# Sums over partitions in the attention heads: from TensorE to GpSimd, with GpSimd's short operations moved to VectorE

## The chip, the cores and the metric

The kernel runs on one core of a Trainium2 chip. The metric is the device time of one execution in microseconds (us); the median of several runs is given, and one more execution was profiled. The engines are TensorE (PE, matrix products), VectorE (DVE), ScalarE (ACT), GpSimd (POOL) and SyncE (SP, which issues most DMA transfers). Each has its own queue of instructions, worked off in order, and waits on the others through semaphores.

## The reference

One layer of a hybrid encoder step, for 512 prompt frames and 64 sample frames (T = 576 in all), in float32. What the change touches is the normalisation of queries and keys in eight attention heads of 128 channels, and the inverse roots of the other norms:

```python
def rmsnorm(x, g):
    y = xf * lax.rsqrt(jnp.mean(xf * xf, axis=-1, keepdims=True) + EPS) * g
...
hn = rmsnorm(x, g_norm1)
proj = hn @ w_in
q, k, v, gb, gc, hc = jnp.split(proj, ...)
q = rmsnorm(q.reshape(B, T, N_HEADS, HEAD_DIM), g_q)
k = rmsnorm(k.reshape(B, T, N_HEADS, HEAD_DIM), g_k)
...
o_attn = stick_breaking_blocks(q, k_all, v_all, P)
u = gc * hc
o_conv = gb * conv3(u)
mix = concat([rmsnorm(o_attn, g_attn_out), rmsnorm(o_conv, g_conv_out)])
x = x + mix @ w_out
x = x + (silu(h2 @ w_gate) * (h2 @ w_up)) @ w_down
```

## The kernel before

Activations lie with channels on the 128 partitions and frames along the row. The 576 frames are worked on in two halves of 288 (`HALVES`, `HALF`). For precision each float32 operand of a product is split into a high and a low part (`split`, line 221: a cast on ScalarE, then a subtraction on VectorE), and a product is three matmuls (`step`, line 210). A product over D = 2048 channels for one half is 16 steps of three matmuls (`product`, line 215). After each step a clock of the program ticks (`pipe.tick()`), and work that was put off until that tick is issued (`Pipeline`, line 66): a generator that yields n goes on n ticks later.

The program has the input stage, then the eight heads (`head`, line 805), then two groups of the convolution in the plain form, the rest in a form with fewer products, the output projection and the feed-forward part. A head projects q, k and v one after the other (`project`, line 489), each for both halves. `norm_evac` (line 619) takes a half of q or k out of PSUM: it multiplies by the row scale R1 into `E` (line 637), squares it on ScalarE (line 640), splits the square, and 13 ticks later (16 for k, 6 and more in head 0) sums it over the partitions by two matmuls with a matrix of ones (`channel_sums`, lines 468 to 472), so that each partition has the sum. `rsqrt_mean` (lines 456 to 466) makes the inverse root of it: the mean plus epsilon on VectorE (461), Ln and Exp on ScalarE (462, 463), and one Newton step of three VectorE operations (464 to 466). Line 629 then scales `E`, and the result is split for the score matmuls.

When both halves of k are there, `attend` (line 660) starts 15 ticks later: scores into the tiles `z` (679), softplus (653 to 656), masks (688), block sums (691, 696), cumulative sums by triangular matmuls, weights (717, 719), the values' product `po` (747), the same for the sample frames with short operations on 64 columns (752 to 758), and at the end the squares of the head's output are added into `acc_a` (`add_squares`, line 504). The masks, block sums, short operations and the adding of squares are on GpSimd. The tile `sq` has two buffers, `hl` (which the split square uses) two.

The weights of the next products are split two products ahead (`next_weight`, line 194; lines 175 and 176); the one numbered 2 is split by GpSimd. In head 0 the evacuation of both halves of q and of k comes at one time, since the row scale R1 is only then known.

TensorE's order is the program's, written by hand. The order on ScalarE, VectorE and GpSimd within the heads is made by the framework's planner from the program's order and its own estimate of costs.

`rsqrt_mean` is also called for the scale of the heads' output (`head_forms`), for that of the groups (`group_scale`) and for the second norm (`row_scale2`), two halves each.

Of the kernel before, what the change touches and what calls it, by code (L numbers as in the profile page):

```python
# [3 lines left out]

# [6 lines left out]
F32 = mybir.dt.float32  # L11
# [5 lines left out]
P = 128  # L17
# [77 lines left out]
def tile_hybrid_stream_step(  # L95
# [89 lines left out]
    def split_weight(lo_eng):  # L185
        raw = raws[len(ready)]
        n = specs[len(ready)][1] * specs[len(ready)][2]
        hi, lo = weight_split(len(ready))
        for a in range(0, n, 1024):
            weight_parts(raw, hi, lo, a, a + 1024, lo_eng)  # L190
# [3 lines left out]
    def next_weight():  # L194
        i = pos[0]
        pos[0] += 1
        end = first_out if i < first_out else first_block
        while len(raws) < min(i + 2, end):
            load_weight()
        while len(ready) < min(i + 2, end):  # L200
            split_weight(nc.gpsimd if i == 2 else nc.vector)
        while len(raws) < min(i + 3, end):
            load_weight()
        out = ready[i]
        ready[i] = None
        return out
# [18 lines left out]
    def parts(name):  # L225
        t = tmp.tile([P, 2, HALF], F32R, tag="hl", name=name)
        return t[:, 0], t[:, 1]
# [225 lines left out]

    hpool.release()

    def rsqrt_mean(dst, src, n, width, ms=None, t=None):
        if ms is None:
            ms = tmp.tile([P, HALF], F32, tag="ms", name="ms", bufs=1)[:, :width]
            t = tmp.tile([P, HALF], F32, tag="t", name="t", bufs=1)[:, :width]
        y = tmp.tile([P, HALF], F32, tag="y", name="y")[:, :width]  # L460
        nc.vector.tensor_scalar(out=ms, in0=src, scalar1=1.0 / n, scalar2=EPS, op0=ALU.mult, op1=ALU.add)
        nc.scalar.activation(out=y, in_=ms, func=AF.Ln)
        nc.scalar.activation(out=y, in_=y, func=AF.Exp, scale=-0.5)
        nc.vector.tensor_tensor(out=t, in0=y, in1=y, op=ALU.mult)
        nc.vector.scalar_tensor_tensor(out=t, in0=t, scalar=-0.5, in1=ms, op0=ALU.mult, op1=ALU.mult)
        nc.vector.scalar_tensor_tensor(out=dst, in0=t, scalar=1.5, in1=y, op0=ALU.add, op1=ALU.mult)

    def channel_sums(src_hi, src_lo, a, b, name):
        ps = misc(name)[:, : b - a]
        mm(ps, oner, src_hi, start=True, stop=False)  # L470
        mm(ps, oner, src_lo, start=False, stop=True)
        return ps
# [28 lines left out]
            else:  # L501
                defer.append((evac, ps, a, b))

    def add_squares(acc, src, first):
        if first:
            nc.scalar.activation(out=acc, in_=src, func=AF.Square)
        else:
            sq = tmp.tile([P, HALF], F32, tag="sq", name="sqm")
            nc.scalar.activation(out=sq, in_=src, func=AF.Square)
            nc.gpsimd.tensor_tensor(out=acc, in0=acc, in1=sq, op=ALU.add)  # L510

    turns = {}

# [53 lines left out]
    def group_scale(acc, dst, rows_of):  # L567

        four = cpool.tile([P, 2, 2, HALF], F32R, tag="uc", name="sqg")
        for i, (a, b) in enumerate(HALVES):  # L570
            sh, sl = four[:, i, 0], four[:, i, 1]
            split(sh, sl, acc[:, a:b])
            yield rows_of
            ss = channel_sums(sh, sl, a, b, "ssg")
            ms, t = (tmp.tile([P, HALF], F32, tag=tag, name=tag + "g") for tag in ("r", "sq"))
            rsqrt_mean(dst[:, a:b], ss, 8 * P, HALF, ms, t)
            yield rows_of

    acc_a = rpool.tile([P, T], F32, tag="R", name="acc_a", bufs=2)
# [39 lines left out]
    def norm_evac(name, gcol, dst_f, dst_hi, dst_lo, first, after=None):  # L619
        E = t1.tile([P, T], F32, tag="E", name=f"E{name}", bufs=2)  # L620

        def rest(a, b, sh, sl):
            if first:
                lags[0] += 4
            yield 6 + lags[0] if first else 16 if after else 13
            ss = channel_sums(sh, sl, a, b, "ss")
            r = tmp.tile([P, HALF], F32, tag="r", name="r")
            rsqrt_mean(r, ss, P, HALF)
            nc.vector.scalar_tensor_tensor(out=dst_f[:, a:b], in0=E[:, a:b], scalar=gcol, in1=r,
                                           op0=ALU.mult, op1=ALU.mult)  # L630
            e = min(b, TP)
            split(dst_hi[:, a:e], dst_lo[:, a:e], dst_f[:, a:e])
            if after and b == T:
                pipe.spawn(after)

        def evac(ps, a, b):
            nc.vector.tensor_tensor(out=E[:, a:b], in0=ps, in1=R1[:, a:b], op=ALU.mult)
            sq = tmp.tile([P, HALF], F32, tag="sq", name="sq")
            sh, sl = parts("sq")
            nc.scalar.activation(out=sq, in_=E[:, a:b], func=AF.Square)  # L640
            split(sh, sl, sq)
            pipe.spawn(rest(a, b, sh, sl))

        return evac

# [14 lines left out]
    def attend(h, st):  # L660
# [20 lines left out]
        for b in (2, 1, 0):  # L681
            parts = (2, 3) if b == 2 else (b,)
            w = full[b]
            for i in parts:
                scores(i)
            softplus(pr[b][:, :w], z[b][:, :w], pr[b][:, :w])
            for i in parts:
                nc.gpsimd.tensor_tensor(out=pb[i][:, :P], in0=pb[i][:, :P], in1=m01, op=ALU.mult)
            split(ph[b][:, : width[b]], pl[b][:, : width[b]], pr[b][:, : width[b]])
            if b == 2:  # L690
                nc.gpsimd.tensor_tensor(out=pb[2][:, P:], in0=pb[2][:, P:], in1=pb[3], op=ALU.add)
                s1h = t1.tile([P, 256], F32R, tag="s1h", name="s1h")
                s1l = t1.tile([P, 256], F32R, tag="s1l", name="s1l")
                split(s1h, s1l, pb[2])
            if b == 1:
                nc.gpsimd.tensor_tensor(out=pb[1][:, P:], in0=pb[1][:, P:], in1=pb[2], op=ALU.add)
                s0h = t1.tile([P, 384], F32R, tag="s0h", name="s0h")
                s0l = t1.tile([P, 384], F32R, tag="s0l", name="s0l")
                split(s0h, s0l, pb[1])
# [49 lines left out]

        sp = t1.tile([P, T], F32, tag="pr0", name="sp")  # L750
        softplus(sp[:, :320], zc, sp[:, :320])
        nc.gpsimd.tensor_tensor(out=sp[:, 256:320], in0=sp[:, 256:320], in1=s01, op=ALU.mult)
        sh = t1.tile([P, T], F32R, tag="ph0", name="sph")
        sl = t1.tile([P, T], F32R, tag="pl0", name="spl")
        sums = sp[:, 320:]
        nc.gpsimd.tensor_copy(sums[:, 192:256], sp[:, 256:320])
        for b in (2, 1, 0):
            nc.gpsimd.tensor_tensor(out=sums[:, b * TS : (b + 1) * TS], in0=sums[:, (b + 1) * TS : (b + 2) * TS],
                                    in1=sp[:, (b + 1) * TS : (b + 2) * TS], op=ALU.add)
        split(sh, sl, sp)  # L760
        yield 18
# [16 lines left out]
        nc.scalar.copy(out=o_attn[h][:, TP:], in_=os_[:, TS:P])  # L778
        for a, b in HALVES:
            yield 3  # L780
            add_squares(acc_a[:, a:b], o_attn[h][:, a:b], h == 0)

    def values(h, st, Ev):
        yield 5
# [1063 lines left out]
```

## Time and profile before

| | us |
|---|---|
| median of 3 runs | 2372.15 |
| lowest and highest of them | 2371.21, 2373.49 |
| the profiled execution's own time | 2373.26 |
| its span, from the first to the last instruction | 2371.6 |

The mean granted TensorE clock in the profiled execution is 0.999 of full speed.

In rows of a timeline the first number is the start and the second the length in us. In rows of groups the two numbers behind the bar are the busy time of the group in us and the mean of one instruction in ns, and behind the second bar stands the idle time of the engine just before them with what ended it. Matmuls overlap one another in their pipeline: a row says 0.29 us for one of 288 columns, while a new one starts about every 0.13 us.

### The profile page before, as it was taken

The page shows a single profiled execution, that of the slowest core. Times are in us where ns is not written, and L with a number is a line of the kernel's source. Part 1 is how long each engine was busy: PE and PEld are TensorE (multiplying, and loading weights), DVE is VectorE, ACT ScalarE, POOL GpSimd, SP SyncE. Part 2 cuts the span into 40 slices and gives each one's busy share as a digit, 9 for nine tenths or more (in the row PEclk, how much of TensorE's full clock was granted, in tenths as well). Part 3 has the DMA queues.
Part 4 walks back from the last instruction along what each step waited for, and adds up shares of the span by engine and source line. Part 5 has one row for each costly group of instructions (what it writes and reads, how often), then busy time and mean ns, then how long its engine had stood idle before and what let it go on. Part 6 is the DMA issues. An engine that isn't in the chain of part 4 may idle for free.

```text
span 2371.6 us, 44043 instructions
## 1 busy us (share of the span) xinstructions
PE 2348.9 (99%) x17653; PEld 2338.0 (99%) x17653; DVE 1927.6 (81%) x2892; ACT 1166.2 (49%) x2083; POOL 290.5 (12%) x386
## 2 busy tenths in 40 slices
PE   8999999999999999999999999999999999999999
PEld 8999999999999999999999999999999999999999
DVE  7868776788887889888888888888888778887876
ACT  6656655444444555444444444444444444444444
POOL 2111111332111230000000000000000002431211
PEclk9999999999999999999999999999999999999999
DMA  8465554683368654444444444444444936886642
GB/s 259 127 179 165 138 148 111 219 263 118 109 235 220 195 166 147 140 152 135 138 152 136 138 152 137 137 152 137 137 152 132 359 112 213 224 225 199 205 131 82
DMA packets 563845, 395.75 MB, mean 167 GB/s; under 512 B 67006, under 2 KB 552760, under 8 KB 563640
## 3 DMA queue, kind: packets, MB, share of 16 engines
q1 hardware_dynamic: 554296, 376.39, 50.6%
q0 software_dynamic: 8624, 16.22, 3.4%
q8 instruction: 138, 2.26, 0.4%
q14 instruction: 67, 0.55, 0.1%
q10 hardware_dynamic: 720, 0.33, 0.0%
HBM read 301.45 MB, written 91.44 MB: 166 GB/s over the span
## 4 chain that ended last, share of the span: by engine, by line
PE 90%; DVE 5%; DMA 2%; ACT 2%; issue 1%; POOL 0%; ACTq 0%; SPq 0%; DVEq 0%; POOLq 0%
PE psy L1532 34%; PE psw L1532 17%; PE pj L213 12%; PE psx L1532 8%; PE psy L1036 6%; PE pjo L213 4%; PE psw L1036 3%; PE psx L1036 2%; DMA raw_a<-in_w_down_dram 1%; DVE whl L223 1%; PE po L747 1%; PE z L679 1%; DVE whl L1008 0%; PE os L777 0%; DMA raw_a<-in_w_in_dram 0%
## 5 line engine op out<-in xcount | busy, mean ns | idle before, releaser
L1532 PE MATMUL psy<-h_s,whl 128*128 128x288 f32 x2787 | 413.5, 295 | 0.3 <-ACT part L1542 0.3
L213 PE MATMUL pj<-x,whi 128*128 128x288 f32 x1856 | 389.9, 297 | 0.3 <-DVE x L356 0.2
L1532 PEld LDWEIGHTS psy<-h_s,whl 128*128 128x128 f32 x2787 | 384.8, 189 | 0.6 <-ACT part L1542 0.5
L223 DVE TENSOR_TENSOR whl<-raw_a,whl 128x1024 fp32r<-128x1024 f32 (+4 forms) x296 | 321.1, 1086 | 61.3 <-ACT whl L222 60.4
L1532 PE MATMUL psw<-t,whl 128*128 128x288 f32 x2400 | 348.3, 295 | 0.0
L1532 PEld LDWEIGHTS psw<-t,whl 128*128 128x128 f32 x2400 | 327.5, 188 | 0.0
L222 ACT CAST whl<-raw_a 128x1024 fp32r<-128x1024 f32 (+4 forms) x296 | 267.8, 906 | 115.2 <-issue 35.4
L213 PEld LDWEIGHTS pj<-x,whi 128*128 128x128 f32 x1856 | 304.1, 189 | 1.5 <-DVE x L356 1.0
L213 PE MATMUL pj<-x,wlo 128*128 128x288 f32 x928 | 274.1, 295 | 0.1
L223 DVE TENSOR_TENSOR whl<-raw_b,whl 128x1024 fp32r<-128x1024 f32 (+5 forms) x190 | 201.6, 1061 | 69.2 <-ACT whl L222 68.1
L222 ACT CAST whl<-raw_b 128x1024 fp32r<-128x1024 f32 (+5 forms) x190 | 165.1, 871 | 167.8 <-issue 73.4
L1542 ACT COPY part<-psy 128x288 f32<-128x288 f32 x242 | 96.6, 399 | 281.4 <-PE psy L1532 279.6
L1532 PE MATMUL psy<-b22m,whl 128*128 128x288 f32 x1212 | 183.3, 295 | 0.2 <-ACT part L1542 0.2
L1532 PE MATMUL psy<-t2t,whl 128*128 128x288 f32 x1212 | 182.9, 294 | 0.0
L213 PEld LDWEIGHTS pj<-x,wlo 128*128 128x128 f32 x928 | 174.5, 188 | 0.7 <-DVE wlo L423 0.3
L1532 PE MATMUL psx<-h_s,whl 128*128 128x288 f32 x1185 | 173.6, 294 | 0.0
L1532 PEld LDWEIGHTS psy<-b22m,whl 128*128 128x128 f32 x1212 | 168.2, 188 | 0.4 <-ACT part L1542 0.4
L1532 PEld LDWEIGHTS psy<-t2t,whl 128*128 128x128 f32 x1212 | 167.9, 188 | 0.0
L1532 PEld LDWEIGHTS psx<-h_s,whl 128*128 128x128 f32 x1185 | 162.3, 188 | 0.0
L222 ACT CAST whl<-s 128x1024 fp32r<-128x1024 f32 (+5 forms) x81 | 72.2, 892 | 102.2 <-PE psw L1532 100.9
L1311 POOL DMA_DIRECT2D hid_dram<-form x3 | 2.3, 751 | 947.6 <-DVE form L223 947.6
L1532 PE MATMUL psy<-t,whl 128*128 128x288 f32 x576 | 107.7, 297 | 0.0
(471 smaller groups left out, 4408.7 us busy)
## 6 DMA issues: line engine op xcount, KB each, us to landing
hid_dram<-form SPq DMA_DIRECT2D x147, 288.0 KB, 2.3
raw_a<-in_w_in_dram SPq DMA_DIRECT2D x41, 1024.0 KB, 5.8
raw_a<-in_w_gate_dram SPq DMA_DIRECT2D x22, 1024.0 KB, 6.0
raw_a<-in_w_up_dram SPq DMA_DIRECT2D x22, 1024.0 KB, 5.7
raw_b<-in_w_gate_dram SPq DMA_DIRECT2D x22, 1024.0 KB, 6.7
raw_b<-in_w_up_dram SPq DMA_DIRECT2D x22, 1024.0 KB, 7.0
h_s<-hid_dram SPq DMA_DIRECT2D x10, 2016.0 KB, 12.5
raw_a<-in_w_out_dram SPq DMA_DIRECT2D x16, 1024.0 KB, 5.6
```

What stands on the lines that cost most here:

```text
L213: mm(ps, w_[:, k, csl], x_, start=(k == 0 and n == 0), stop=(k == nk - 1 and n == 2))
L222: nc.scalar.copy(out=hi, in_=src)
L223: (lo_eng or nc.vector).tensor_tensor(out=lo, in0=src, in1=hi.bitcast(F32), op=ALU.subtract)
L679: mm(zb[i], a_[:, kk], b_[:, q0:TP], start=(n == 0), stop=False, skip_group_check=True)
L747: mm(po[:, i * P : 512], a_[:, i, :], b_[:, : 512 - i * P], stop=(i == 0 and n == 2), **kw)
L1036: mm(ps, whl[:, w_, j, :], x_, start=(start and j == 0 and q == 0), stop=(j == m - 1 and q == 2), skip_group_check=True)
L1311: q.dma_start(out=hid_dram[fp][2 * n - 2 : 2 * n].rearrange("f p t -> p f t"), in_=t.bitcast(F32))
L1532: mm(ps, whl[:, w_, j, :], x_, start=(start and j == 0 and q == 0), stop=(j == len(xs_) - 1 and q == 2), skip_group_check=True)
L1542: nc.scalar.copy(out=t, in_=st["y"])
```

## The change

The sum of squares over the partitions in `norm_evac` is no longer made from split squares by two matmuls: GpSimd's `partition_all_reduce` adds the squares of a half (128 partitions by 288 columns, float32) over the partitions, right after ScalarE's square, and writes the sum to every partition of an SBUF tile in the tag `hl`. The split of the square is left out. The lags of 13, 16 and 6 ticks stay.

The masks, the block sums, the short operations on sample frames, and the adding of squares at the end of a head go from GpSimd to VectorE, and so does the one weight split. The memset of `ws` stays on GpSimd, and so does the adding of squares for the convolution groups.

`rsqrt_mean` leaves out line 461: Ln takes the sum itself, with the scale 1/n and epsilon as a bias, and the Newton step is written with the sum in place of the mean. Its first operation becomes one with a scalar between the two operands.

```diff
-            split_weight(nc.gpsimd if i == 2 else nc.vector)
+            split_weight(nc.vector)
...
+    epsc = rpool.tile([P, 1], F32, name="epsc")
+    nc.vector.memset(epsc, EPS)
+
-    def rsqrt_mean(dst, src, n, width, ms=None, t=None):
-        if ms is None:
-            ms = tmp.tile([P, HALF], F32, tag="ms", name="ms", bufs=1)[:, :width]
+    def rsqrt_mean(dst, src, n, width, t=None):
+        if t is None:
             t = tmp.tile([P, HALF], F32, tag="t", name="t", bufs=1)[:, :width]
         y = tmp.tile([P, HALF], F32, tag="y", name="y")[:, :width]
-        nc.vector.tensor_scalar(out=ms, in0=src, scalar1=1.0 / n, scalar2=EPS, op0=ALU.mult, op1=ALU.add)
-        nc.scalar.activation(out=y, in_=ms, func=AF.Ln)
+        nc.scalar.activation(out=y, in_=src, func=AF.Ln, scale=1.0 / n, bias=epsc)
         nc.scalar.activation(out=y, in_=y, func=AF.Exp, scale=-0.5)
-        nc.vector.tensor_tensor(out=t, in0=y, in1=y, op=ALU.mult)
-        nc.vector.scalar_tensor_tensor(out=t, in0=t, scalar=-0.5, in1=ms, op0=ALU.mult, op1=ALU.mult)
+        nc.vector.scalar_tensor_tensor(out=t, in0=y, scalar=-0.5 / n, in1=y, op0=ALU.mult, op1=ALU.mult)
+        nc.vector.scalar_tensor_tensor(out=t, in0=src, scalar=n * EPS, in1=t, op0=ALU.add, op1=ALU.mult)
         nc.vector.scalar_tensor_tensor(out=dst, in0=t, scalar=1.5, in1=y, op0=ALU.add, op1=ALU.mult)
...
-    def add_squares(acc, src, first):
+    def add_squares(acc, src, first, eng=nc.gpsimd):
...
-            nc.gpsimd.tensor_tensor(out=acc, in0=acc, in1=sq, op=ALU.add)
+            eng.tensor_tensor(out=acc, in0=acc, in1=sq, op=ALU.add)
...
-        def rest(a, b, sh, sl):
+        def rest(a, b, ss):
...
-            ss = channel_sums(sh, sl, a, b, "ss")
...
         def evac(ps, a, b):
             nc.vector.tensor_tensor(out=E[:, a:b], in0=ps, in1=R1[:, a:b], op=ALU.mult)
             sq = tmp.tile([P, HALF], F32, tag="sq", name="sq")
-            sh, sl = parts("sq")
             nc.scalar.activation(out=sq, in_=E[:, a:b], func=AF.Square)
-            split(sh, sl, sq)
-            pipe.spawn(rest(a, b, sh, sl))
+            ss = tmp.tile([P, HALF], F32, tag="hl", name="ss")
+            nc.gpsimd.partition_all_reduce(ss, sq, P, bass_isa.ReduceOp.add)
+            pipe.spawn(rest(a, b, ss))
...
-                nc.gpsimd.tensor_tensor(out=pb[i][:, :P], in0=pb[i][:, :P], in1=m01, op=ALU.mult)
+                nc.vector.tensor_tensor(out=pb[i][:, :P], in0=pb[i][:, :P], in1=m01, op=ALU.mult)
...
-                nc.gpsimd.tensor_tensor(out=pb[2][:, P:], in0=pb[2][:, P:], in1=pb[3], op=ALU.add)
+                nc.vector.tensor_tensor(out=pb[2][:, P:], in0=pb[2][:, P:], in1=pb[3], op=ALU.add)
...
-                nc.gpsimd.tensor_tensor(out=pb[1][:, P:], in0=pb[1][:, P:], in1=pb[2], op=ALU.add)
+                nc.vector.tensor_tensor(out=pb[1][:, P:], in0=pb[1][:, P:], in1=pb[2], op=ALU.add)
...
-        nc.gpsimd.tensor_tensor(out=sp[:, 256:320], in0=sp[:, 256:320], in1=s01, op=ALU.mult)
+        nc.vector.tensor_tensor(out=sp[:, 256:320], in0=sp[:, 256:320], in1=s01, op=ALU.mult)
...
-        nc.gpsimd.tensor_copy(sums[:, 192:256], sp[:, 256:320])
+        nc.vector.tensor_copy(sums[:, 192:256], sp[:, 256:320])
         for b in (2, 1, 0):
-            nc.gpsimd.tensor_tensor(out=sums[:, b * TS : (b + 1) * TS], in0=sums[:, (b + 1) * TS : (b + 2) * TS],
+            nc.vector.tensor_tensor(out=sums[:, b * TS : (b + 1) * TS], in0=sums[:, (b + 1) * TS : (b + 2) * TS],
...
-            add_squares(acc_a[:, a:b], o_attn[h][:, a:b], h == 0)
+            add_squares(acc_a[:, a:b], o_attn[h][:, a:b], h == 0, nc.vector)
```

`group_scale` calls the shorter `rsqrt_mean` with one scratch tile less.

More of the change, by code (lines that the diff above doesn't have):

```diff
@@ L574, in group_scale @@
             ss = channel_sums(sh, sl, a, b, "ssg")
-            ms, t = (tmp.tile([P, HALF], F32, tag=tag, name=tag + "g") for tag in ("r", "sq"))
-            rsqrt_mean(dst[:, a:b], ss, 8 * P, HALF, ms, t)
+            t = tmp.tile([P, HALF], F32, tag="sq", name="sqg")
+            rsqrt_mean(dst[:, a:b], ss, 8 * P, HALF, t)
             yield rows_of
```

1 line of the change is left out of this document (added).

## The prediction

> **What bounds the kernel now.** I read the page first, then the time per head, then the engines inside one head, then single instructions.
>
> ```profile
> span 2371.6 us, 44043 instructions
> PE 2348.9 (99%) x17653; PEld 2338.0 (99%) x17653; DVE 1927.6 (81%) x2892; ACT 1166.2 (49%) x2083; POOL 290.5 (12%) x386
> ```
>
> TensorE (PE) is the bound of the whole. The change touches the eight heads, about 46 to 420 us. One head is read off the chain of waits, from the score matmuls of one head to those of the next (first column start, second length, us), and the busy times from the view of stretches over five such heads:
>
> ```profile
> 258.03 1.23 PE z L679 x6
> ...
> 305.82 1.23 PE z L679 x6
> ```
>
> ```profile
> 258.03:305.82 47.79, 47.79 (x357) 47.43 (x357) 36.02 (x70) 28.97 (x62) 7.41 (x14) 1.00 0.52 140
> ...
> sum 238.97, PE 238.97 PEld 237.16 DVE 181.34 ACT 145.48 POOL 34.10; mean PE 47.79 PEld 47.43 DVE 36.27 ACT 29.10 POOL 6.82
> ```
>
> A head is 47.8 us and PE is busy in all of it, at the full clock (1.00). VectorE (DVE) works 36.3 us of it and idles 11.5, GpSimd (POOL) works 6.8. So a matmul taken out of a head is worth its full slot, and DVE has 11.5 us a head before it takes PE's place.
>
> **The two engines get in each other's way.** These rows of the timeline carry the forecast (start, length, engine, line):
>
> ```profile
> 49.77 4.99 POOL L176 TENSOR_TENSOR wlo<-raw_a,whi 128x1024 fp32r<-128x1024 f32 x2 [10.02 <-ACT whi L175]
> ...
> 50.70 0.46 DVE L461 TENSOR_SCALAR ms<-ss 128x288 f32<-128x288 f32 x1 [1.98 <-PE ss L471]
> ...
> 52.49 2.58 DVE L464 TENSOR_TENSOR t<-y 128x288 f32<-128x288 f32 x1
> ...
> 57.98 0.45 DVE L464 TENSOR_TENSOR t<-y 128x288 f32<-128x288 f32 x1
> ```
>
> ```profile
> 293.46 1.22 DVE L176 TENSOR_TENSOR wlo<-raw_a,whi 128x1024 fp32r<-128x1024 f32 x1
> ...
> 293.81 1.53 POOL L510 TENSOR_TENSOR acc_a<-acc_a,sqm 128x288 f32<-128x288 f32 x1 [5.64 <-ACT sqm L509]
> ...
> 294.59 1.06 DVE L464 TENSOR_TENSOR t<-y 128x288 f32<-128x288 f32 x1
> ```
>
> L464 multiplies two SBUF operands. Alone it takes 0.45 us. At 52.49, with two GpSimd instructions under way until 54.76, it took 2.58 us and ended at 55.07, just behind them. At 293.81 the GpSimd add met a running VectorE subtraction, took 1.53 us, and the next L464 then waited for the add (1.06 us). L461, which reads PSUM, ran at 50.70 inside the same GpSimd work in its usual 0.46 us. So a VectorE instruction with two SBUF inputs and a GpSimd instruction run one after the other, each waiting for the whole of the other. A GpSimd sum over partitions reads SBUF too, and here it is four times a head.
>
> The Trainium skill ("SBUF — State Buffer", section "SBUF: two separate sides") says the same: the port pair the two engines share is an exclusive lock held for a full instruction, against VectorE operations with two SBUF inputs. The rows above agree for GpSimd's elementwise operations; no run so far shows it for a sum over partitions.
>
> **How much of VectorE's work can be held up.** From the groups by line over those five heads, the rows whose operation reads PSUM or has one input only:
>
> ```profile
> L461 DVE TENSOR_SCALAR ms<-ss 128x288 f32<-128x288 f32 x20 | 9.1, 453 | 3.2 <-PE ss L471 3.2
> L656 DVE SCALAR_TENSOR_TENSOR pr<-z,pr 128x384 f32<-128x384 f32 (+1 forms) x15 | 8.4, 583 | 0.7 <-ACT pr L655 0.7
> ...
> L717 DVE SCALAR_TENSOR_TENSOR z<-z,acA 128x128 f32<-128x128 f32 x20 | 6.0, 298 | 11.0 <-PE z L726 9.0 <-PE z L732 1.9
> ...
> L785 DVE STREAM_TRANSPOSE Ev<-Ev 128x576 f32<-128x576 f32 x6 | 4.7, 779 | 0.2
> L832 DVE TENSOR_TENSOR Ev<-pj,R 128x288 f32<-128x288 f32 x10 | 4.5, 453 | 6.5 <-PE pj L213 6.5
> L637 DVE TENSOR_TENSOR Ek<-pj,R 128x288 f32<-128x288 f32 x10 | 4.5, 453 | 1.1 <-PE pj L213 1.1
> L637 DVE TENSOR_TENSOR Eq<-pj,R 128x288 f32<-128x288 f32 x10 | 4.5, 448 | 0.0
> ...
> L710 DVE STREAM_TRANSPOSE kb<-kf 128x576 f32<-128x576 f32 x5 | 3.9, 778 | 0.2
> ...
> L803 DVE STREAM_TRANSPOSE kcT<-cK 128x512 f32<-128x512 f32 x5 | 3.5, 709 | 2.2 <-PE zs L705 2.2
> ...
> L769 DVE TENSOR_TENSOR ws<-cz,zc 128x320 f32<-128x320 f32 x5 | 2.4, 479 | 0.0
> ```
>
> They sum to 51.5 us, 10.3 a head. The other 36.3 - 10.3 = 26.0 us a head read two SBUF operands.
>
> **The change part by part.**
>
> *Matmuls out.* Each of the 32 sums (8 heads, q and k, two halves) loses two matmuls. In the timeline the pair starts at 50.24 and the next matmul behind it at 50.50:
>
> ```profile
> 50.24 0.29 PE L470 MATMUL ss<-sq,oner 128*128 128x288 f32 x1
> ...
> 50.50 0.29 PE L213 MATMUL pjz<-x,whi 128*128 128x288 f32 x1
> ```
>
> 0.26 us a pair, 1.04 a head, 32 x 0.26 = 8.3 us: all that PE can gain. The 32 casts on ScalarE that go with them lie beside PE (ScalarE 29.1 of 47.8 us) and count nothing.
>
> *VectorE out and in.* Per head it loses four subtractions and four L461, and takes what GpSimd did:
>
> ```profile
> L223 DVE TENSOR_TENSOR sq<-sq 128x288 fp32r<-128x288 f32 x20 | 11.5, 577 | 2.4 <-ACT sq L222 2.3
> ...
> L607 DVE TENSOR_TENSOR o_ob<-o_ob 128x288 f32<-128x288 f32 x5 | 2.3, 455 | 0.1
> ...
> L770 DVE SCALAR_TENSOR_TENSOR ws<-ws,acA 128x64 f32<-128x64 f32 x5 | 1.1, 213 | 0.0
> ```
>
> ```profile
> L688 POOL TENSOR_TENSOR pr<-pr,acA 128x128 f32<-128x128 f32 x20 | 9.6, 501 | 20.4 <-DVE pr L656 20.4
> L510 POOL TENSOR_TENSOR acc_a<-acc_a,sqm 128x288 f32<-128x288 f32 x10 | 9.1, 911 | 75.5 <-ACT sqm L509 75.5
> L758 POOL TENSOR_TENSOR sp<-sp 128x64 f32<-128x64 f32 x15 | 5.0, 330 | 1.2
> ```
>
> Out: 4 x 0.577 + 4 x 0.453 = 4.1 us. In, priced by VectorE's rows of the same width: four masks and one add of 128 columns at 0.30 (L717), one add of 256 at 0.42 (between L717 and L607), five of 64 at 0.21 (L770), two adds of 288 at 0.455 (L607): 3.9 us. VectorE stays at 36.1 us a head, but its two-input work goes from 26.0 to 26.0 - 2.3 + 3.9 = 27.6. The squaring L464 becomes one of the same kind and length. The weight split that head 0 gave GpSimd (4.99 us) is two VectorE instructions of 1.2 us; it ends L464's wait of 2.1 us, so nought. The six other inverse roots (heads' and groups' scales, R2) lose one L461 each, 6 x 0.45 = 2.7 us at most; VectorE has other work there and I count zero.
>
> *The sum over partitions.* No row has it. The nearest is L510, one GpSimd pass over 128x288 in 0.91 us: the lower bound, since every column is read and written at least once. From above, GpSimd's slowest operation here is a power worked out in software:
>
> ```profile
> 38.53 1.21 POOL L441 TENSOR_TENSOR rst<-ssr,nhalf 128x5 f32<-128x5 f32 x1 [12.10 <-DVE ssr L439]
> ```
>
> 1.21 us for 5 columns is 0.24 a column, 70 us for 288: the upper bound. I take a value near L510's end, since it only adds: 128 rows are folded to one in seven halvings, at a pass of 0.91 us each 6.4 us. I call it X = 6.4, an estimate.
>
> The Trainium skill's figure that speaks against it ("GPSIMD Engine Reference", section "3.2 Cross-partition — where GPSIMD wins") is 247.7 us for a reduction along partitions of 128x2048, so 34.8 us for 288 columns by an estimate from that page, and it is for another instruction; by it a head would be 27.6 + 4 x 34.8 = 167 us and the time about 3330 us. No trace shows it yet.
>
> *What waits.* GpSimd's queue in a head holds nothing else but a memset, so nothing is stuck behind the sums there. Who waits is VectorE, by the lock, and behind it ScalarE's casts, the weight splits and PE. If lock and work pack without a gap, a head is 27.6 + 4 x 6.4 = 53.2 us. If instead the sums fall at chance, only the share of a head without two-input work, (47.8 - 26.0)/47.8 = 46%, is free to run beside them, and a head is 47.8 - 1.0 + 0.54 x 25.6 = 60.6 us. ScalarE's and VectorE's order is the planner's, and where it puts the readers of a sum I can't see; a reader put too early holds its whole engine. I take the middle, 56.9, 9.1 above today, for eight heads 73 us. Cover and lateness: without the lock the sums would mostly hide, since the program leaves time for them:
>
> ```profile
> 268.36 0.44 ACT L640 ACTIVATE sq<-Eq 128x288 f32<-128x288 f32 x1 [1.89 <-DVE Eq L637]
> ...
> 291.33 0.45 ACT L640 ACTIVATE sq<-Ek 128x288 f32<-128x288 f32 x1
> ```
>
> ```profile
> 273.31 0.46 DVE L461 TENSOR_SCALAR ms<-ss 128x288 f32<-128x288 f32 x1 [0.44 <-PE ss L471]
> ...
> 299.11 0.44 DVE L461 TENSOR_SCALAR ms<-ss 128x288 f32<-128x288 f32 x1
> ```
>
> From the square's end to L461 there are 4.5 us for the first half of q and 7.3 for the last of k. In head 0 four squares come together, the first at 46.7; the last L461 is at 62.6, and the view of waits shows PE already short of k there:
>
> ```profile
> 46.73 0.81 ACT L640 ACTIVATE sq<-Eq 128x288 f32<-128x288 f32 x2 [6.81 <-DVE Eq L637]
> ...
> 62.60 0.45 DVE L461 TENSOR_SCALAR ms<-ss 128x288 f32<-128x288 f32 x1
> ```
>
> ```profile
> PE z L679 <- ACT kh L222: 2.0, 1, 2.0
> ```
>
> Four sums in a row, 25.6 us, in these 16 us make head 0 late by some 10 us, about as much as the others lose; it is counted as one of the eight.
>
> **Sum.** The profiled execution took 2373.3 us (span 2371.6 and 1.7 around it), the median of the runs is 2372.15. 2373.3 + 73 = 2446; against the median 2445. I forecast 2445, slower.
>
> **Rivals.** (a) *The sum is short*, X of about 3 us or less: 27.6 + 12 fits into 46.8 us, it lies in VectorE's idle time, and the heads shrink by the matmuls: 2372 - 8.3 = 2364. For it: GpSimd passes of 0.9 us, and 4.5 to 7.3 us of room. Against: three passes are few for 128 rows, and a head's chain has VectorE steps behind each other. The point from which it turns is 0.54 x 4X = 1.0 + what VectorE's idle time absorbs, near X = 3 to 4. (b) *The lock doesn't hold for this instruction*, or X is just at that point: then only q's first half is late (6.4 against 4.5 us) and head 0 waits (25.6 us of sums in a room of about 16 us), giving back what the matmuls gave: 2368 to 2377. For it: the lock is shown for elementwise operations only. (c) *The sum goes column by column* and GpSimd itself is the bound, above X = 12, where 4X exceeds 47.8 us. At X = 16 a head is 27.6 + 64 = 91.6 us, plus 44 each: 2372 + 350 = 2722. For it: the power's 0.24 us a column; against: a power is dear arithmetic, a sum isn't.
>
> **Chances.** Forecast (lock, X about 4 to 12, 2380 to 2600 by the same two formulas): 0.52. (a) 0.25. (b) 0.08. (c) 0.15. What a measurement of this kernel tells from no change is 0.2%, 4.7 us. So faster 0.25, same 0.08, slower 0.67. The range must take in (a), since the other sign holds a quarter: 2362 to 2600; it leaves out (c) and little else. The likeliest case alone: 2380 to 2600.
>
> **What would show it.** The row of the sum on GpSimd, 32 times, gives X directly: 6.4 expected. VectorE's two-input rows (L464's successor, the weight splits of 1.2 us) should have means some us above their 0.45 and 1.2 where a sum runs, and PSUM readers (the multiplication out of PSUM, 0.45) should not. A head between score matmuls should be about 57 us, with PE waiting for VectorE or ScalarE; the time behind 450 us should be unchanged. Wrong would be: X under 3 us with heads of 46.8 us; or X of 6 us with VectorE's means unchanged, which would mean that there is no lock for this instruction; or GpSimd busy in all of a head.

## The result and the profile after

| | before | after |
|---|---|---|
| median of 4 runs (us) | 2372.82 | 2406.2 |
| lowest and highest | 2371.21, 2374.73 | 2404.51, 2409.49 |
| ratio after / before | | 1.014, 95% interval 1.0128 to 1.0153 |
| span of the profiled execution | 2371.6 | 2405.3 |

The change makes the kernel slower by 33.4 us. The forecast had the sign, and more than twice the size (73 us); that the sign was right was luck, as the account of the prediction below shows. First the page of the kernel after:

```profile
span 2405.3 us, 43819 instructions
...
PE 2356.3 (98%) x17589; PEld 2344.3 (97%) x17589; DVE 1939.5 (81%) x2927; ACT 1160.1 (48%) x2051; POOL 304.5 (13%) x314
```

TensorE still bounds it, with 64 matmuls fewer, as meant; but it has 33.7 us more of span and only 7.4 us more of busy time. So most of the loss is time in which TensorE stands still, and some is matmuls that are each a little longer. Where it lies can be read off the first and last starts of the matmuls of one line (view by source line; the three numbers before the range are the shortest, median and longest duration in ns). Before, the convolution and the feed-forward part:

```profile
L1036 PE MATMUL psy<-x,whl x624: 292/294/398, 486.0 to 691.0; 128*128 128x288 f32 x156
...
L1036 PE MATMUL psy<-forms,whl x384: 290/294/399, 691.1 to 782.5; 128*128 128x288 f32 x192
```

```profile
L1532 PE MATMUL psy<-h_s,whl x2787: 290/294/445, 884.1 to 2366.2; 128*128 128x288 f32 x200
```

After:

```profile
L1037 PE MATMUL psy<-x,whl x624: 292/294/608, 507.0 to 719.7; 128*128 128x288 f32 x156
...
L1037 PE MATMUL psy<-forms,whl x384: 293/297/370, 719.8 to 810.2; 128*128 128x288 f32 x192
```

```profile
L1533 PE MATMUL psy<-h_s,whl x2787: 291/297/442, 911.9 to 2399.8; 128*128 128x288 f32 x200
```

Three stretches lose. The convolution starts at 507.0 instead of 486.0: the heads lose **21.0 us**. From there to the products with `forms` it takes 212.8 us instead of 205.1: **7.7 us**. The feed-forward part runs 1487.9 us instead of 1482.1: **5.8 us**, with a median matmul of 297 ns instead of 294. They sum to 34.5; between the second and the third stretch it gains 0.9 (193.0 to 192.1).

The disputed price has its row now, in the groups by line of GpSimd (kernel after, 40 to 460 us):

```profile
L642 POOL PARTITION_ALL_REDUCE ss<-sq x32 | 74.1, 2317 | 273.3 <-ACT sq L640 261.9 <-DVE o_ob L609 5.8 <-DVE t L467 4.9
```

X is 2.3 us, not 6.4. By the forecast's own rule that is rival (a), "the sum is short", whose time was 2364. And one head does run as (a) says: here is the seventh to the eighth head's scores in the view of stretches (the columns as before):

```profile
375.79:422.42 46.63, 46.63 (x349) 46.27 (x349) 34.70 (x69) 26.16 (x54) 9.75 (x8) 1.00 0.48 125
```

46.6 us instead of 47.8, TensorE without a gap. The other heads don't. This table gives the start of each head's first score matmul, from the timelines (us):

| head | 0 | 1 | 2 | 3 | 4 | 5 | 6 | 7 |
|---|---|---|---|---|---|---|---|---|
| before | 68.9 | 111.4 | 161.7 | 209.5 | 257.3 | 305.1 | 352.9 | 400.7 |
| after | 71.3 | 113.9 | 178.3 | 227.5 | 275.3 | 325.9 | 375.0 | 421.7 |

14.1 of the 21 us are lost in one place, between heads 1 and 2 (64.4 us instead of 50.3), 2.4 before the first scores, and 2.8, 1.4 and 1.4 in three others. The waits of TensorE from 40 to 520 us (sum in us, times, longest) name the places:

```profile
PE po L748 <- ACT vh L223: 12.1, 2, 11.1
PE psy L1037 <- ACT whl L1006: 5.5, 1, 5.5
PE z L680 <- ACT kh L223: 5.3, 1, 5.3
PE os L778 <- issue: 4.9, 3, 2.2
```

The wait of 11.1 us is for ScalarE's cast of the values, `vh`. What ScalarE did meanwhile stands in the timeline after:

```profile
141.74 3.41 DVE L177 TENSOR_TENSOR wlo<-raw_a,whi 128x1024 fp32r<-128x1024 f32 x2 [0.31 <-ACT whi L176]
...
142.15 2.66 POOL L642 PARTITION_ALL_REDUCE ss<-sq  x1 [7.45 <-ACT sq L640]
...
144.84 0.54 ACT L464 ACTIVATE y<-ss,epsc 128x288 f32<-128x288 f32 x1 [1.46 <-POOL ss L642]
...
150.87 2.05 POOL L642 PARTITION_ALL_REDUCE ss<-sq  x1 [4.23 <-ACT sq L640]
...
152.95 0.53 ACT L464 ACTIVATE y<-ss,epsc 128x288 f32<-128x288 f32 x1 [2.25 <-POOL ss L642]
153.52 0.44 ACT L465 ACTIVATE y<-y 128x288 f32<-128x288 f32 x1
153.87 0.49 ACT L223 CAST vh<-vtok 128x384 fp32r<-128x384 f32 x1
...
154.41 0.58 PE L748 MATMUL po<-ph,vh 128*128 128x256 f32 x1 [11.05 <-ACT vh L223]
```

Read it from below. The cast of `vh` needs nothing but its data, which had long been there (the transfer was issued at 133.1, and such a one takes 2.6 to 4.2 us); it stands in ScalarE's queue behind the logarithm (L464) of a sum that GpSimd finished only at 152.92, and that logarithm stands directly behind the square that feeds the sum. ScalarE's queue is worked off in order, so it waited. The view of ScalarE's waits (46 to 425 us) shows it for nearly every sum; before, the logarithm waited for VectorE's step instead:

```profile
ACT y L464 <- POOL ss L642: 59.9, 31, 3.5
```

```profile
ACT y L462 <- DVE ms L461: 13.5, 12, 3.7
```

The two waits of 2.2 us at `os` (L778, heads 4 and 5) are the same thing on VectorE: the first step of `ws`, which `os` reads, stands there behind a step of the root (L466) that needs the logarithm of a sum, at 318.03 and at 368.69 us.

Before, the matmuls were what held the logarithm back: TensorE's order is written by hand and placed them 13 to 16 ticks behind the square, so the planner had to put the logarithm late. Without them the `yield` still moves the instruction in the program's text, but no dependency does, and the planner pulls it forward.

### The profile page after: what moved, and what is told of

The parts are those of the page before. It is cut to its first block, busy times and chain, and to the rows that moved or that the text cites. A ratio compares the mean times of both kernels' runs of the same rounds, so it can differ in the third digit from the quotient of the medians.

```text
span 2405.3 us, 43819 instructions
## 1 busy us (share of the span) xinstructions
PE 2356.3 (98%) x17589; PEld 2344.3 (97%) x17589; DVE 1939.5 (81%) x2927; ACT 1160.1 (48%) x2051; POOL 304.5 (13%) x314
## 4 chain that ended last, share of the span: by engine, by line
PE 88%; DVE 4%; ACT 3%; DMA 2%; POOL 1%; issue 1%; SPq 0%; ACTq 0%; DVEq 0%; POOLq 0%
PE psy L1533 34%; PE psw L1533 17%; PE pj L214 9%; PE psx L1533 9%; PE psy L1037 6%; PE pjo L214 4%; PE psw L1037 3%; PE psx L1037 2%; POOL ss L642 1%; DMA raw_a<-in_w_in_dram 1%; DVE wlo L177 1%; DMA form_dram<-hf 1%; PE po L748 1%; ACT whi L176 1%; DMA raw_a<-in_w_down_dram 0%
## 5 line engine op out<-in xcount | busy, mean ns | idle before, releaser
L177 DVE TENSOR_TENSOR wlo<-raw_a,whi 128x1024 fp32r<-128x1024 f32 (+1 forms) x74 | 99.6, 1363 | 14.9 <-ACT whi L176 13.3
```

The lines of the kernel that those rows point to most:

```text
L177: lo_eng.tensor_tensor(out=lo[:, a:b], in0=raw[:, a:b], in1=hi[:, a:b].bitcast(F32), op=ALU.subtract)
```

## Experiments

Thirteen kernels ran besides the two. The first four tell the parts of the change apart: theory A is the order of the sum's readers, B the lock between VectorE and GpSimd, C VectorE's added load.

**The new inverse root alone** (e1_root: before, with the new `rsqrt_mean`, and its constant tile)

```diff
+    epsc = rpool.tile([P, 1], F32, name="epsc")
+    nc.vector.memset(epsc, EPS)
...
-        nc.vector.tensor_scalar(out=ms, in0=src, scalar1=1.0 / n, scalar2=EPS, op0=ALU.mult, op1=ALU.add)
-        nc.scalar.activation(out=y, in_=ms, func=AF.Ln)
+        nc.scalar.activation(out=y, in_=src, func=AF.Ln, scale=1.0 / n, bias=epsc)
...
```

> The kernel before with the shorter inverse root alone. All theories: no sum on GpSimd, so no wait of ScalarE on GpSimd for it; 46 VectorE steps of 0.45 us less, beside other work. 2366 to 2374 us. Over 2380 would mean that the new root itself costs time (Ln waits for the matmul's sum directly).

2379.94 us, ratio 1.0028 (1.0018 to 1.0039): no theory had foreseen a loss here. The heads are as before; the last of them starts its scores at 400.5. The feed-forward part is what got longer:

```profile
L1533 PE MATMUL psy<-h_s,whl x2787: 291/297/406, 885.1 to 2372.3; 128*128 128x288 f32 x200
```

1487.2 us and 297 ns, as in the changed kernel, though that code is untouched. What the edit does change there is addresses: the new tile takes 32 bytes per partition, and the addresses that the build gives show some hundred tiles behind it moved by 32 bytes. The first part of the convolution, up to `forms`, is longer as well, 207.0 us instead of 205.1.

**The constant in a place that was free** (e10_root_pad: e1_root, with the constant in a column of a tile that the kernel holds and doesn't use, so nothing behind it moves; e11_pad: the changed kernel with the same)

```diff
-    lpad.tile([P, 8], F32, name="lpad_t")
+    lpad_t = lpad.tile([P, 8], F32, name="lpad_t")
...
-    epsc = rpool.tile([P, 1], F32, name="epsc")
+    epsc = lpad_t[:, :1]
```

> The kernel before plus only the new inverse root, as in e1_root, but the constant tile of 32 bytes per partition is a column of a tile that the kernel before already holds and doesn't use, so that no tile behind it moves by 32 bytes. Theory D (the 5.8 us of the feed-forward part come from the moved addresses): feed-forward length back at 1481 to 1484 us (e1_root 1488.4), time 2364 to 2373 us, ratio 0.997 to 1.000. Rival E (the new root itself, or the swapped places of t and y, lengthens it): as e1_root, 2378 to 2382 us, ratio 1.002 to 1.004.

> The changed kernel with the constant in that same unused column. Theory D: feed-forward length 1481 to 1484 us instead of 1489, all else as after: 2398 to 2402 us. Rival E: 2405 to 2408 us.

e10_root_pad: 2371.98 us, ratio 0.9997 (0.9988 to 1.0005). e11_pad: 2395.02 us, 1.0094 (1.0078 to 1.0109). The feed-forward rows, of e10_root_pad first, of e11_pad below:

```profile
L1533 PE MATMUL psy<-h_s,whl x2787: 290/294/442, 882.9 to 2364.9; 128*128 128x288 f32 x200
```

```profile
L1533 PE MATMUL psy<-h_s,whl x2787: 290/294/398, 905.9 to 2385.6; 128*128 128x288 f32 x200
```

1482.0 and 1479.7 us, 294 ns both: theory D. The 5.8 us are the moved tiles; the new root itself costs and gains nothing that can be told. The three kernels that hold a new tile (e1_root, e7_paced, the changed one) run this part in 1485.5 to 1487.9 us, all others in 1479.7 to 1482.6. In e11_pad the first part of the convolution lost 3.6 us less than in the changed kernel (209.2 instead of 212.8 us), and the heads happened to lose 2 us less, which is why it is below the 2398 to 2402 expected.

**The GpSimd sum alone** (e2_sum: before, with GpSimd's sum in place of the split and the matmuls; the short operations stay on GpSimd)

```diff
-            sh, sl = parts("sq")
             nc.scalar.activation(out=sq, in_=E[:, a:b], func=AF.Square)
-            split(sh, sl, sq)
-            pipe.spawn(rest(a, b, sh, sl))
+            ss = tmp.tile([P, HALF], F32, tag="hl", name="ss")
+            nc.gpsimd.partition_all_reduce(ss, sq, P, bass_isa.ReduceOp.add)
+            pipe.spawn(rest(a, b, ss))
```

> The kernel before with the sum on GpSimd alone; short operations stay on GpSimd, the long root stays. Theory A (order: the planner puts the readers of a sum right behind the square, ScalarE or VectorE stand for about 2 us at each of 32 sums, and casts that TensorE needs come late): 2385 to 2410 us, with ScalarE's or VectorE's waits on GpSimd's sum at some 60 us. Theory B (the lock between GpSimd's sum and VectorE's two-input operations): also slower, 2380 to 2395, but with VectorE's two-input rows longer by up to 2 us at each sum. Theory C (VectorE is overfilled by the short operations it takes over): 2364 to 2372.

2460.75 us, ratio 1.0368 (1.0351 to 1.0385): far worse than the whole change, and beyond what any of the theories gave. A stretch of GpSimd's timeline in this kernel, about one head:

```profile
265.87 1.57 POOL L511 TENSOR_TENSOR acc_a<-acc_a,sqm 128x288 f32<-128x288 f32 x2 [7.21 <-issue]
...
273.19 0.65 POOL L688 TENSOR_TENSOR pr<-pr,acA 128x128 f32<-128x128 f32 x1
279.89 1.99 POOL L641 PARTITION_ALL_REDUCE ss<-sq  x1 [6.05 <-issue]
...
303.59 0.31 POOL L752 TENSOR_TENSOR sp<-sp,acA 128x64 f32<-128x64 f32 x1 [7.01 <-DVE wlo L177]
...
311.45 1.99 POOL L641 PARTITION_ALL_REDUCE ss<-sq  x1 [6.05 <-ACT xs_out L223]
```

Each time GpSimd goes from elementwise work to a sum it stands for some 6 us (5.9 to 6.5 from the third head on), and from a sum to elementwise work for some 7 (6.8 to 7.5, once 10.0). Between two sums it doesn't, and a memset in between does nothing. The short operations on `sp`, which come behind such a change, are then late for ScalarE's cast of them, and that for TensorE (waits of TensorE from 40 to 560 us, then of ScalarE from 46 to 425 us):

```profile
PE cz L763 <- ACT sph L223: 45.8, 6, 16.0
```

```profile
ACT sph L223 <- POOL sp L758: 19.7, 6, 4.7
```

With four changes a head, each head from the third on is 7 to 10 us longer. So the moving of the short operations to VectorE, which looks like a side matter of the change, is what makes the sum bearable at all.

**The short operations alone** (e3_short: before, with masks, block sums, short operations, squares and the weight split on VectorE; the sums as before)

```diff
-                nc.gpsimd.tensor_tensor(out=pb[i][:, :P], in0=pb[i][:, :P], in1=m01, op=ALU.mult)
+                nc.vector.tensor_tensor(out=pb[i][:, :P], in0=pb[i][:, :P], in1=m01, op=ALU.mult)
...
...
-            add_squares(acc_a[:, a:b], o_attn[h][:, a:b], h == 0)
+            add_squares(acc_a[:, a:b], o_attn[h][:, a:b], h == 0, nc.vector)
```

> The kernel before with the short operations and the one weight split on VectorE, sums still by matmuls. Theories A and B: within 5 us of before, 2367 to 2377, since VectorE idles 11.5 us a head and loses the waits for GpSimd. Theory C: 2390 to 2410.

2370.54 us, ratio 0.9991 (0.9982 to 1.0001). Theory C falls: VectorE has room for it. Two heads' scores in the chain of waits are 47.79 us apart, as before:

```profile
257.05 1.23 PE z L679 x6
...
304.84 1.23 PE z L679 x6
```

**GpSimd's change of code in the changed kernel.** There all sums come first and elementwise work follows only behind the heads, so one change is left over, and the convolution waits for it: ScalarE's casts of `hf` wait for these additions, and the cast of the convolution's weights `whl` stands behind them (kernel after: the timeline of GpSimd, then the view by line of the instructions of L560):

```profile
473.97 0.74 POOL L527 DMA_DIRECT2D mix_dram<-mx  x1 [9.47 <-DVE mx L525]
481.95 5.33 POOL L560 TENSOR_TENSOR o_oa<-o_oa 128x288 f32<-128x288 f32 x5 [7.24 <-issue]
```

```profile
L560 POOLq MODIFY_POOL_CONFIG  x2: 37/37/37, 474.8 to 474.8; - x2
```

The addition at 481.95 waited 7.24 us for nothing that the profile shows, behind an instruction of GpSimd's queue that changes its configuration. The Trainium skill ("GPSIMD Engine Reference", section "2.1 Instruction dispatch") says that code can be loaded into GpSimd at run time by this instruction and that the first call to a freshly loaded routine costs about 6 us that no instruction of the profile shows; the 6.05 us before the sums of e2_sum agree, and the runs add that it recurs with every change and is some 7 us on the way back. To test it, e12_early adds to e11_pad one addition of one column behind the last sum, so that the change falls into the last head:

```diff
+            if last and b == T:
+                nc.gpsimd.tensor_tensor(out=lpad_t[:, 1:2], in0=ss[:, :1], in1=ss[:, 1:2], op=ALU.add)
             pipe.spawn(rest(a, b, ss))
```

> e11_pad plus one GpSimd addition of one column, queued directly behind the last sum over partitions, so that GpSimd's change from sums to elementwise work falls into the last head. Theory F (the 7.2 us before GpSimd's first addition after the heads are a change of its code): GpSimd's wait of 7.2 us moves to that addition, the convolution's start comes 5 to 8 us sooner, 2391 to 2396 us. Rival G (the wait belongs to the operand or to the addition of 128x288 itself): the wait stays where it was, 2398 to 2402 us, as e11_pad.

2392.97 us, ratio 1.008 (1.0067 to 1.0094). Its timeline of GpSimd, in two parts:

```profile
422.84 0.18 POOL L644 TENSOR_TENSOR lpad_t<-ss 128x1 f32<-128x1 f32 x1 [8.38 <-issue]
```

```profile
475.98 3.48 POOL L560 TENSOR_TENSOR o_oa<-o_oa 128x288 f32<-128x288 f32 x3 [0.54 <-DVE hf L224]
```

Theory F: the wait went with the code, to an addition of one column, and L560 starts as soon as its operand is there. From the convolution's first matmul to its 600th it now takes 84.1 us, as before the change (84.4), where e11_pad had 88.5 and the changed kernel 91.7. So 4.4 us are the change of code; the 3.2 between the last two went with the constant's place alone. The median fell by 2 us only, since this kernel's heads lost 2.6 us more than e11_pad's.

**The order of the readers.** e7_paced gives the logarithm a dependency on TensorE again: a matmul of one column that reproduces epsilon stands where the sum's matmuls stood, ScalarE copies it, and the logarithm takes it as its bias.

```diff
+            eps = misc("eps")[:, :1]
+            mm(eps, ident, epsc, start=True, stop=True)
+            eps_s = tmp.tile([P, 1], F32, tag="eps", name="eps_s")
+            nc.scalar.copy(out=eps_s, in_=eps)
-            rsqrt_mean(r, ss, P, HALF)
+            rsqrt_mean(r, ss, P, HALF, eps=eps_s)
```

> The changed kernel, but Ln's epsilon comes through a one-column matmul and a one-column copy on ScalarE issued at the old lag, so that the planner can't put the readers of a sum before that tick. Theory A: ScalarE's waits on the sums fall from 60 us to under 15, the stalls of TensorE in the heads go, and the time is 2360 to 2372, at or below before. Theory B or C: 2395 to 2410, as changed.

2389.54 us, ratio 1.0073 (1.0058 to 1.0088): half of the loss is gone, the heads lose 7.8 us instead of 21.0, and ScalarE's wait on `ss` has left the head of its list. It is not the 2360 to 2372 that theory A gave. What is left of TensorE's waits:

```profile
PE po L752 <- ACT vh L223: 4.2, 1, 4.2
PE z L684 <- ACT kh L223: 3.7, 1, 3.7
```

The first is the same place in head 1, and ScalarE's timeline says why:

```profile
145.20 0.38 ACT L223 CAST qh<-qf 128x224 fp32r<-128x224 f32 x1 [1.50 <-DVE qf L634]
145.49 0.51 ACT L223 CAST vh<-vtok 128x384 fp32r<-128x384 f32 x1
```

Here the cast of the values stands behind that of the next head's query, which waits for the whole chain of the root. In the kernel before, `vh` stood ahead of `qh` at this place. In the changed kernel it stands behind the two logarithms shown above. e13_order_early takes the planner away: in the heads, ScalarE and VectorE follow the order of the program's text (otherwise as e12_early).

```diff
     head_mode = ExitStack()
+    head_mode.enter_context(tc.manual_schedule(engines={mybir.EngineType.Activation, mybir.EngineType.DVE}))
```

> e12_early with the order of ScalarE's and VectorE's instructions in the heads as the program's text gives it (with its delays counted in projection steps), not as the planner sorts them. Theory A (the 21 us of the heads are readers of a sum standing ahead of casts that TensorE needs): the logarithms come 6 to 17 projection steps behind the sum, ScalarE no longer waits for sums, heads of 46.6 to 48 us, time 2362 to 2378 us. Rival H (the sums are late wherever their readers stand, because VectorE holds them up): heads stay above 49 us, 2388 us or more. Third way: the text's order is bad in other places, TensorE's waits then name other tiles.

2494.27 us, ratio 1.0504 (1.049 to 1.0519), the slowest of all, and the third way of the expectation. Its first rows of TensorE's waits:

```profile
PE po L750 <- ACT ph L223: 63.9, 14, 9.1
PE po L747 <- DMA vtok<-vt_dram: 13.9, 6, 4.1
```

ScalarE's longest list is now queues behind VectorE (`kh` 38.9 us) and behind a transfer (`vh` 37.9 us), not sums. That tells that the order alone can cost over 100 us with the same operations, but not what the right order gives; it is no test of theory A.

Three kernels then refined the pacing: constant and early change of code as in e12_early, the matmul in fp32r on two columns, no new tile; e15_pace0 with the lags as they were, e16_pace1 and e17_pace3 with lags 1 and 3 ticks shorter (the last lines below are those of e17_pace3).

```diff
+            eps = misc("eps")[:, :2]
+            mm(eps, oner, rpad_t[:, :2], start=True, stop=True)
+            c = 4 + turn_e[0] % 4
+            turn_e[0] += 1
+            eps_s = lpad_t[:, c : c + 1]
+            nc.scalar.copy(out=eps_s, in_=eps[:, :1])
...
-            yield 6 + lags[0] if first else 16 if after else 13
+            yield 6 + lags[0] if first else 13 if after else 10
```

> e12_early with each sum's logarithm held back by a two-column fp32r matmul of the constant (sum over 128 partitions of a 128th of it) at the place where the sum's two matmuls stood in the kernel before, and a one-column ScalarE copy of its result. Theory A (order): no PE wait on the casts vh and kh in heads 3 to 7, these heads 46.6 to 47.0 us; the first three, whose order the planner still sorts otherwise than before, 0 to 8 us over; time 2362 to 2375 us. Rival H (the sums are late wherever their readers stand): heads of 48 us or more throughout, 2385 us or more.

> e15_pace0 with that matmul one projection step earlier, which makes up for the added copy. Theory A: the values' cast stands ahead of the next head's query cast in more heads, so the early heads lose less: 2360 to 2372 us. If order is left to chance by any such shift: some head still waits 4 us or more on a cast, 2372 to 2385 us.

> e15_pace0 with that matmul three projection steps earlier. Theory A: as e16_pace1, 2360 to 2375 us, with the sum still landed in time (it takes 2.3 us, the matmul stands 10 and 13 steps behind the square). Rival: with less lag the roots wait for the sums again, ScalarE waits on ss in its list, over 2375 us.

2379.91 us (1.0034, 1.0022 to 1.0047), 2390.37 us (1.0075, 1.0061 to 1.0088) and 2394.15 us (1.009, 1.0074 to 1.0105). In e15_pace0 the scores from head 2 to head 7 are 47.2, 47.2, 47.2, 47.6 and 47.2 us apart, a little over A's 46.6 to 47.0 and under H's 48, and no cast is waited for there, as A says and H doesn't; the heads lose 6.8 us in all instead of 21.0. Heads 0 and 1 still wait for `kh` and for `vh` (4.0 and 4.3 us). The time is over the 2375 that A allowed and under H's 2385. The two shorter lags are worse, against A's expectation: other heads then wait 2.5 us for `vl` or 1.4 us for `vh`, presumably since each shift makes the planner sort all of it anew.

**All but the sum** (e14_nosum_pad: short operations, weight split and new root, its constant in the free column; the sums as two matmuls)

> All of the change but the sum over partitions: short GpSimd operations and the weight split on VectorE, the new root, its constant in the unused column; the sums stay two matmuls. e3_short gave 0.9991 and e10_root_pad 0.9997. If the two add up: 2366 to 2371 us, ratio 0.998 to 0.9995, heads of 47.7 us. If VectorE's time became scarce by the two together, heads of 48 us or more and 2373 us or more.

2368.67 us, ratio 0.9984 (0.9975 to 0.9992). The two parts add up, and this is faster than both kernels.

**The sum where the order is right** (e18_late: e15_pace0, but heads 0 to 2, in two of which a cast was still late, keep the matmuls; a sum of one column in head 0 loads GpSimd's code early)

```diff
+                if first and b == T:
+                    nc.gpsimd.partition_all_reduce(lpad_t[:, 1:2], sq[:, :1], P, bass_isa.ReduceOp.add)
...
-        q_evac = norm_evac("q", gqs, st["qf"], st["qh"], st["ql"], h == 0)
+        q_evac = norm_evac("q", gqs, st["qf"], st["qh"], st["ql"], h == 0, gp=h >= 3)
```

> e15_pace0 with the sums of heads 0 to 2 as two matmuls again (the heads whose casts still stood behind the next query's chain) and GpSimd's sum from head 3 on; a sum of one column in head 0 brings GpSimd's code early. Theory A (what was left of the loss in e15_pace0 is the start of head 0 and the one stall of 4.3 us in head 1): heads 0 to 2 as in e14_nosum_pad, heads 3 to 7 of 46.8 to 47.3 us, no stall over 1 us, 2363 to 2368.5 us, ratio 0.996 to 0.9985. Rival H (the sum itself keeps a head from getting shorter): heads 3 to 7 of 47.7 us or more, 2369 us or more.

2365.78 us, ratio 0.9968 (0.9957 to 0.998), within theory A's numbers. The chain of waits between two heads with GpSimd's sum, and the whole of TensorE's waits from 40 to 480 us:

```profile
253.26 1.23 PE z L702 x6
...
300.47 1.22 PE z L702 x6
```

```profile
PE po L770 <- DVE vl L224: 0.9, 1, 0.9
PE ss L475 <- DVE t L470: 0.8, 1, 0.8
```

47.21 us a head instead of 47.8, with no stall of more than 1 us, and a sum that still takes 2.32 us in the mean. So a sum on GpSimd pays, by 0.6 us a head, once its readers are held back, its code is loaded early and no tile moves. It beats both kernels, and perhaps e14_nosum_pad (their intervals overlap, and they ran beside different runs of before).

## Why the prediction went wrong

Two steps failed. The sum's price X was put at 6.4 us and is 2.3; and the order of the sum's readers, named in the forecast, was left out of its sum, and cost most of the 21.0 us that the heads lost. With X = 2.3 the forecast's own rule gives 2364, faster than before: that the kernel is slower, as forecast, was luck.

*What bounds it, and the gain of the matmuls.* Right. A head without stalls took 46.63 us, 1.16 less than 47.79, where 1.04 was forecast.

*VectorE's load.* Right: 34.7 us in that head where 36.1 was forecast, and e3_short shows that the added work and the weight split cost nothing.

*The sum's price.* Wrong, the first failed step: X was put at 6.4 us from seven passes of 0.91 us, and measured 2.3 (2.0 where nothing disturbs it, the median of e2_sum's sums being 1.99). The bounds 0.91 and 70 held it. Between ends so far apart the number of passes was a guess about how the sum is done, and the whole forecast of 73 us stood on it. (The formula for sums that fall at chance would, with 2.3, give 51.8 us a head and some 2404 in all. That this is near 2406 is chance: it prices the lock, and the lock is not what cost the time.)

*The lock.* Right in kind, small in size. VectorE's weight splits in the heads, before and after:

```profile
L176 DVE TENSOR_TENSOR wlo<-raw_a,whi 128x1024 fp32r<-128x1024 f32 x48 | 59.0, 1238 | 2.6 <-ACT whi L175 2.5
```

```profile
L177 DVE TENSOR_TENSOR wlo<-raw_a,whi 128x1024 fp32r<-128x1024 f32 x47 | 67.1, 1438 | 12.4 <-ACT whi L176 12.0
```

47 x 0.20 = 9.4 us over eight heads, while the readers of PSUM kept their 0.45 us as expected. How long a sum holds the path shows in a copy of 64 columns on VectorE, 0.20 us alone, that started 0.25 us into the sum at 150.87 shown above (timeline after):

```profile
151.12 1.11 DVE L757 COPY sp<-sp 128x64 f32<-128x64 f32 x1
```

It ended at 152.23, so it was let go about 1.2 us behind the sum's start, with 0.9 us of the sum to come. In ten of the kernels 68 operations with two inputs start inside a sum that nothing else disturbs (1.97 to 2.06 us) and are held up; all come free 1.0 to 1.2 us behind its start, and none that starts later than 0.9 us is held up. So this sum holds the path for about its first 1.1 us, a little over half of it. The Trainium skill ("SBUF — State Buffer", section "SBUF: two separate sides") has one instruction block the other for the whole of it; the sum's rows disagree with that, the elementwise rows in the prediction agree. The copy has one input only, and the prediction had counted such work as free. In the heads shown by e18_late VectorE's idle time takes these delays up: they carry the same sums without a stall.

*Rival (a).* Its condition came true (X under 3) and its time did not: 2364 against 2406.2. The rule by which the forecast went over from one case to the other, whether sums and work pack into a head, was not what decided. Three things did, in the three stretches that lost 21.0, 7.7 and 5.8 us:

1. The readers of the sum, the second failed step and most of the 21.0 us. The prediction said that the planner's order can't be seen and that a reader put too early holds its whole engine, and then put no price on it. It could have been seen that the two matmuls were the only thing that kept the logarithm late; a delay that is written as a `yield` has force only through an engine whose order is fixed. Shown by e15_pace0 (heads 2 to 7), where 15 us of the heads' loss came back against e12_early, and by e18_late; the rest in heads 0 and 1 is order, too, by the waits named, but no run changed that order and nothing else.
2. GpSimd's change of code, 4.4 of the 7.7 us. Not in the prediction; it held that GpSimd's queue has nothing stuck behind the sums. The same change, ahead of the first sum, stood in the kernel after as a wait of 7.56 us, most of it beside the wait for head 0's squares. Shown by e2_sum and e12_early.
3. Addresses. "The time behind 450 us should be unchanged" was wrong by 12.6 us in all; 5.8 of it are the 32 bytes of the constant. Shown by e1_root, e10_root_pad and e11_pad. The other 3.2 us of the convolution's loss went with the constant's place, too; e1_root alone has 1.5 of them over the same 600 matmuls (85.9 us instead of 84.4), and how the rest comes about is open.

*The six other roots*, counted at zero: right, by e10_root_pad.

*Head 0*, late by some 10 us by the forecast: 2.4 us.

## What to carry to other kernels

An operation that is moved off the engine with the fixed order takes away the pacing of everything that reads its result: look for what else holds those readers back, and give them a cheap dependency if nothing does. Before an operation is moved onto GpSimd, look at what stands next to it in GpSimd's queue, and keep its kinds of work apart in time. A new tile, however small, belongs where it moves no other; a loss in code that was not touched is a reason to look at addresses first.

## What the hardware showed that was not expected

GpSimd's change between a sum over partitions and elementwise work costs some 6 us one way and some 7 us the other (once 8.4, once 10.0), each time.

A sum over partitions of 1.97 us keeps VectorE's two-input operations waiting for its first 1.1 us only.

A shift of the matmuls' operands by 32 bytes lengthened the median matmul in the feed-forward part from 294 to 297 ns, over 1482 us by 5.8. The runs show that it goes with the addresses; by which access it comes about they don't show.

A stall of TensorE costs more than its length. The stretches around the wait of 11.05 us in the kernel after (TensorE's busy time with the number of matmuls, granted clock, DMA share and GB/s):

```profile
141.00:154.00 13.00, 2.36 (x19) 0.73 0.06 19
154.00:161.00 7.00, 5.00 (x18) 0.53 0.31 85
161.00:168.00 7.00, 7.00 (x55) 1.00 0.75 235
```

In stretches of 1 us the clock is at 0.50 from about 147, 3.5 us after TensorE stopped, to 160.5. Some 4.5 us of matmuls fell into that time and cost about 2.3 us more, an estimate from these stretches. With the waits of 11.05 and 1.58 us and less the 1.1 that the head saved, that is 13.8 of the 14.1 us lost between heads 1 and 2. The Trainium skill ("TensorE: Matmul & The Clock Gate", part 1) has the clock at half rate after an idle window of about 3.4 us; the trace agrees with its 3.5. e15_pace0 lost 7.6 us between the same heads by waits of 4.3 and 1.0, with the clock at half from 147.4 to 154.2.
